# A two-layer encoder trunk on one core: activation tables fetched in place, the squares of x four chunks later, and two more matmul steps for two joins

## The chip, the cores and the metric

The kernel runs on one core of one Trainium2 chip. The metric is the device time of one execution in microseconds; less is better. A profile of one execution is read beside it. The engines are named as in the profile: PE multiplies matrices (PEld loads its weights), DVE works on vectors, ACT evaluates activation functions and copies with a scale, POOL works on vectors too, and SP issues most transfers from the chip's memory.

## The reference

The input is one sequence of 512 tokens with 1024 features. Two layers follow each other, and each adds a mixer and then an MLP to the stream x, both in sandwich form:

```
x = x + RMSNorm_post(mixer(RMSNorm_pre(x)))
x = x + RMSNorm_post(mlp(RMSNorm_pre(x)))        mlp(h) = relu(h @ w1)**2 @ w2, hidden 4096
layer 0 mixer: short gated convolution and latent attention with 8 heads, one input and one output projection
layer 1 mixer: u = h @ w_pw1 + b; u = a * sigmoid(g); depthwise convolution, width 31;
               LayerNorm over channels; silu; @ w_pw2 + b
```

All arithmetic is float32 to the outside.

## The kernel before

The activations lie transposed: eight chunks of 128 features on the partitions, tokens along the row. A weight strip of 128x1024 comes in by SP, is split into a rounded part `whi` (ACT, line 224) and a remainder `wlo` (POOL, line 225), and each product takes three matmuls, high by high, high by low and low by high (lines 247 to 249, `mm`), so that one output tile of 128 features takes 8 chunks x 3 = 24 matmuls. Only two raw strips are held at the start, and eight split strips, so SP issues a strip when POOL has finished an older one, and ACT splits one when PE has finished with the strip eight before it.

**The start.** `split_x(j)` loads chunk j of x, multiplies it by its gain on DVE (line 572), splits the product into h (ACT, line 231) and its remainder (DVE, line 234), and has ACT square x for the norm (`square`, line 359); DVE adds the squares up (line 334). `START` interleaves this with the first weight strips. The matmuls don't wait for the norm: PE sums 512-token products in five PSUM banks (`S` has three, `pj` two), and each result is multiplied by R0, the broadcast reciprocal root, when it leaves its bank (line 604). R0 comes from a sum over partitions on PE (line 369), a Newton iteration on DVE (`rstd`, lines 395 to 425), a broadcast on PE (`spread`, line 434) and a copy by ACT (line 596).

**The later stages.** From the first MLP on, the tokens are worked on in two halves, A and B, that are out of step with each other: while one half passes through a join or a norm, in which PE would wait, the other half's matmul steps are pulled forward. The lists `M2` and `M3` give the order by hand. A step is one output tile (24 matmuls); `('down', 'B', 0, 0, 0, 2)` stands for the steps 0 and 1 of a down projection. `hold` and `pace`, called inside a join or a norm, pull the next step from the list, but only as long as it belongs to the other half:

```
        if not steps or steps[0][0] or steps[0][1][1] in ("F", scope["half"]):
            return False
```

So the join `('join', 'A', 0, 3)` can pull the ten steps that stand behind it, eight of up and two of down of half B, and then meets `('pw1', 'A', ...)`, which is its own half's. Pulled steps don't call for convolution work (`fill` returns at once while pulling); every other step gives credit to the convolution taps that DVE works off between other things, 2.6 us for a first down step.

A **join** (`join`) takes the post norm, adds to x, sums squares, takes `rstd`, broadcasts it by `spread` (PE, line 434) and makes the next input h: product on DVE (line 505), rounded copy on ACT (line 231), remainder on DVE (line 234). The **gated units** `pw1` follow (`glu`): two output tiles each, sigmoid of the second (ACT, line 801), product on DVE into u (line 805), which frees the first one's bank. The **norm** (`layer_norm`) first uses up what is left of the convolutions, then sums, broadcasts the mean (line 434), sums squares (line 369), broadcasts the reciprocal root (line 434), and makes h again: product (DVE, line 860), silu (ACT, line 863), rounded copy (ACT, line 231), remainder (DVE, line 234). `pw2` multiplies that.

ACT holds one table of functions at a time; a function that isn't in it needs an ACT_TABLE_LOAD first, which the compiler puts ahead of it. Copy, square and relu appear behind any of the loads in this kernel. To fetch tables early, `join` and `layer_norm` run sigmoid and silu on a 128x1 tile `warm` (lines 502 and 848), which depends on nothing but a memset at the program's start.

The order of each engine's instructions is set by the framework's scheduler from the dependences and its own estimate of durations; for DVE from `M2` on it is the order in which the code was written.

## Time and profile before

| | |
|---|---|
| median of three runs | 1176.1 us (1175.84 to 1176.19) |
| the profiled execution, its own time | 1176.2 us |
| its span from first to last instruction | 1174.4 us |
| PE busy, of the span | 1135.2 us, 97% |
| ACT, DVE, POOL busy | 667.8, 648.6 and 846.6 us |
| mean granted PE clock | 0.991 |

The profiled execution's time agrees with the median to 0.1 us; 1.8 us of it lie outside the span. The page's first part gives busy times by engine. The view of waits names who waited for whom, with the sum, the number and the longest in microseconds. In a timeline, a row has its start, its duration, engine, line, operation and tiles, and in brackets the idle time of the engine ahead of it and what ended that. The view by stretches gives each engine's busy time in a stretch with the number of instructions, then the granted PE clock, the share of the DMA engines and their GB/s.

### The profile page before, as it was taken

What the parts mean: (1) busy time and instruction counts of PE and PEld (TensorE: products, weight loads), DVE (VectorE), ACT (ScalarE), POOL (GpSimd) and SP (SyncE); (2) the same over time, 40 slices, a digit from 0 to 9 for tenths busy, and PEclk for the clock granted to TensorE, in tenths of its full rate; (3) what the DMA queues carried; (4) which work ended last, traced back from release to release, by engine and by line L of the source; (5) the groups of instructions that cost most, each with busy time, mean ns of one, the idle gap of its engine ahead of it and who ended that gap; (6) DMA issues with size and microseconds to landing.
All of it is one profiled execution on the core that took longest, in us unless ns stands there. A gap on an engine that the chain in (4) does not pass through costs nothing.

```text
span 1174.4 us, 22870 instructions
## 1 busy us (share of the span) xinstructions
PE 1135.2 (97%) x8850; PEld 1096.5 (93%) x8850; DVE 648.6 (55%) x1701; ACT 667.8 (57%) x1220; POOL 846.6 (72%) x409
## 2 busy tenths in 40 slices
PE   6999989999999999999999999999999999999995
PEld 4888879999999999899999999899999999999995
DVE  5652699554522124599965265699975272322123
ACT  7521667556845457545566678546467685545352
POOL 4664553148988888688886878698888877877681
PEclk9999999999999999999999999999999999999998
DMA  6421332037655555455554655455555555653431
GB/s 193 157 89 36 97 108 72 1 105 240 200 180 190 188 173 189 135 201 184 179 195 147 200 178 184 139 200 197 197 177 183 179 172 170 197 180 127 156 130 39
DMA packets 55405, 184.00 MB, mean 157 GB/s; under 512 B 6400, under 2 KB 10880, under 8 KB 55296
## 3 DMA queue, kind: packets, MB, share of 16 engines
q1 hardware_dynamic: 54720, 181.86, 46.8%
q8 instruction: 69, 1.13, 0.4%
q10 hardware_dynamic: 576, 0.68, 0.2%
q14 instruction: 40, 0.33, 0.1%
HBM read 180.42 MB, written 2.10 MB: 155 GB/s over the span
## 4 chain that ended last, share of the span: by engine, by line
PE 86%; ACT 4%; DVE 4%; POOL 2%; DMA 2%; issue 1%; POOLq 0%; ACTq 0%; DVEq 0%
PE S L247 22%; PE S L248 21%; PE S L249 21%; PE pj L247 6%; PE pj L248 6%; PE pj L249 6%; POOL wlo L225 2%; DMA raw<-in_w 1%; ACT whi L224 1%; DVE pr L763 1%; PE mi L369 1%; PE mi L434 1%; PE mi L766 1%; PE o L248 1%; DVE s L757 1%
## 5 line engine op out<-in xcount | busy, mean ns | idle before, releaser
L225 POOL TENSOR_TENSOR wlo<-raw,whi 128x1024 fp32r<-128x1024 f32 (+2 forms) x347 | 803.5, 2330 | 258.2 <-ACT whi L224 249.6
L224 ACT ACTIVATE whi<-raw 128x1024 fp32r<-128x1024 f32 (+2 forms) x347 | 355.9, 1031 | 378.0 <-PE S L248 173.1
L247 PE MATMUL S<-h,whi 128*128 128x256 f32 (+3 forms) x1208 | 347.3, 290 | 5.5 <-ACT h L231 3.7
L248 PE MATMUL S<-h,whi 128*128 128x256 f32 (+3 forms) x1208 | 348.4, 289 | 0.0
L249 PE MATMUL S<-h,wlo 128*128 128x256 f32 (+3 forms) x1208 | 348.3, 289 | 0.0
L247 PEld LDWEIGHTS S<-h,whi 128*128 128x128 f32 x1208 | 227.8, 190 | 10.8 <-ACT h L231 4.3
L247 PE MATMUL S<-hid,whi 128*128 128x256 f32 (+2 forms) x824 | 230.3, 282 | 2.3 <-DVE acc L334 1.8
L249 PEld LDWEIGHTS S<-h,wlo 128*128 128x128 f32 x1208 | 229.1, 190 | 3.5
L248 PEld LDWEIGHTS S<-h,whi 128*128 128x128 f32 x1208 | 228.9, 190 | 3.5 <-issue 0.2
L248 PE MATMUL S<-hid,whi 128*128 128x256 f32 (+2 forms) x824 | 230.9, 281 | 0.0
L249 PE MATMUL S<-hid,wlo 128*128 128x256 f32 (+2 forms) x824 | 230.4, 281 | 0.0
L828 DVE SCALAR_TENSOR_TENSOR pj<-u,taps,pj 128x240 f32<-128x240 f32 (+1 forms) x464 | 190.9, 483 | 1.0
L247 PEld LDWEIGHTS S<-hid,whi 128*128 128x128 f32 x824 | 154.8, 189 | 3.3 <-DVE acc L334 2.2
L249 PEld LDWEIGHTS S<-hid,wlo 128*128 128x128 f32 x824 | 155.6, 189 | 0.0
L248 PEld LDWEIGHTS S<-hid,whi 128*128 128x128 f32 x824 | 155.5, 189 | 0.1
L247 PE MATMUL pj<-h,whi 128*128 128x272 f32 (+3 forms) x344 | 105.8, 308 | 11.9 <-ACT h L231 10.2
L248 PE MATMUL pj<-h,whi 128*128 128x272 f32 (+3 forms) x344 | 105.1, 306 | 0.5 <-DVE h L234 0.5
L249 PE MATMUL pj<-h,wlo 128*128 128x272 f32 (+3 forms) x344 | 104.5, 304 | 0.0
L247 PEld LDWEIGHTS pj<-h,whi 128*128 128x128 f32 x344 | 64.9, 189 | 15.7 <-ACT h L231 11.0
L237 DVE TENSOR_TENSOR hid<-S,hid 128x256 fp32r<-128x256 f32 (+2 forms) x102 | 42.8, 420 | 54.3 <-ACT hid L231 54.0
L248 PEld LDWEIGHTS pj<-h,whi 128*128 128x128 f32 x344 | 65.0, 189 | 4.2 <-DVE h L234 1.8
L249 PEld LDWEIGHTS pj<-h,wlo 128*128 128x128 f32 x344 | 65.0, 189 | 2.6
(250 smaller groups left out, 1661.7 us busy)
## 6 DMA issues: line engine op xcount, KB each, us to landing
raw<-in_w SPq DMA_DIRECT2D x256, 512.0 KB, 3.3
raw<-in_pw SPq DMA_DIRECT2D x48, 512.0 KB, 3.4
raw<-in_win SPq DMA_DIRECT2D x16, 512.0 KB, 3.3
x<-in_xT SPq DMA_DIRECT2D x16, 256.0 KB, 4.6
raw<-in_wout SPq DMA_DIRECT2D x8, 512.0 KB, 3.3
raw<-in_wq SPq DMA_DIRECT2D x8, 192.0 KB, 2.3
out<-x SPq DMA_DIRECT2D x8, 120.0 KB, 3.1
out<-x SPq DMA_DIRECT2D x5, 136.0 KB, 1.7
```

The costliest lines, as they stand in the source:

```text
L224: nc.scalar.activation(h, r, AF.Copy)
L225: nc.gpsimd.tensor_tensor(out=lo[:, c0:c1], in0=r, in1=h.bitcast(F32), op=ALU.subtract)
L237: eng.tensor_tensor(out=lo, in0=src, in1=hi.bitcast(F32), op=ALU.subtract)
L247: nc.tensor.matmul(acc, sh, mh, start=i == 0, stop=False)
L248: nc.tensor.matmul(acc, sh, ml, start=False, stop=False)
L249: nc.tensor.matmul(acc, sl, mh, start=False, stop=i == n - 1)
L369: nc.tensor.matmul(s[:, b : b + 1], q[:, sl.start - self.seg.lo : sl.stop - self.seg.lo], one, start=i == 0, stop=i == len(self.parts) - 1,)
L434: nc.tensor.matmul(o[:, sl], r[:, b : b + 1].to_broadcast([bw, P]), ident[:bw, :bw], start=True, stop=True,)
L757: nc.vector.reduce_max(out=mx, in_=S, axis=AX.X)
L763: eng.tensor_scalar(out=pr_, in0=pr_, scalar1=sm, scalar2=None, op0=ALU.mult)
L766: nc.tensor.transpose(tp[:, kb * P : (kb + 1) * P], pr_[:, kb * P : (kb + 1) * P], ident)
L828: nc.vector.scalar_tensor_tensor(out=dst, in0=src, scalar=wk, in1=acc, op0=ALU.mult, op1=ALU.add)
```

## The change

Three edits go together.

1. The tile `warm` is gone. A fetch of a table writes a new small tile and reads one column of a sum or of the mean that was made just ahead of it, so it can't be placed before that value exists.
2. In the start, chunk j's call squares chunk j-4, and the last four are squared behind all chunks; the sum of squares for R0 is therefore issued later, and the splits of x come first.
3. In `M2`, the first down group of half B stands with four steps ahead of `('pw1', 'A', 0, 8)` and four behind, and the first down group of half A in layer 1 likewise around `('pw1', 'B', 0, 8)`; before it was two and six.

```diff
-... ('down', 'B', 0, 0, 0, 2), ('pw1', 'A', 0, 8), ('down', 'B', 0, 0, 2, 8), ...
-... ('down', 'A', 1, 0, 0, 2), ('pw1', 'B', 0, 8), ('down', 'A', 1, 0, 2, 8), ...
+... ('down', 'B', 0, 0, 0, 4), ('pw1', 'A', 0, 8), ('down', 'B', 0, 0, 4, 8), ...
+... ('down', 'A', 1, 0, 0, 4), ('pw1', 'B', 0, 8), ('down', 'A', 1, 0, 4, 8), ...
+LAG = 4
+    def table():
+        return new(sp, "table", 2, 1)
 # join
         bc = rstds(ssq)
-        nc.scalar.activation(warm[0], warm[0], AF.Sigmoid)
+        nc.scalar.activation(table(), ssq.parts[0][:, :1], AF.Sigmoid)
 # split_x
-        s0.square(xs[j].t)
+        if j >= LAG:
+            s0.square(xs[j - LAG].t)
 # behind the loop over START
     settle()
+    for j in range(NC - LAG, NC):
+        s0.square(xs[j].t)
+        settle()
 # layer_norm
         total = spread(mu, seg)
-        nc.scalar.activation(warm[0], warm[0], AF.Silu)
+        nc.scalar.activation(table(), mu[:, :1], AF.Silu)
 # ahead of run(M2)
-    warm.append(new(sp, "warm", 1, 1))
-    nc.vector.memset(warm[0], 0.0)
```

Lines up to 445 are one higher in the changed kernel, those of `join` and `split_x` five, those of the start behind it and of `layer_norm` nine.

On ACT at the program's start, before (its first four rows stand there twice, one set behind the other) and after; `ycat` is the square of the first chunk, `mi` and `o` are scaled chunks, `x3` the second chunk of x:

```order
L502 ACT_TABLE_LOAD
L502 ACTIVATE warm596_2837<-warm596_2837 128x1
L848 ACT_TABLE_LOAD
L848 ACTIVATE warm596_2837<-warm596_2837 128x1
L359 ACTIVATE ycat27_107<-x2_79 128x512
L224 ACTIVATE whi29_110<-raw28_109 128x128
L231 ACTIVATE h10_87<-mi26_104 128x512
```

```order
L567 ACT_TABLE_LOAD
L567 ACTIVATE s11_75<-s11_75 128x1
L360 ACTIVATE ycat37_151<-x2_79 128x512
L225 ACTIVATE whi28_108<-raw27_107 128x128
L232 ACTIVATE h10_87<-mi26_104 128x512
L225 ACTIVATE whi28_108<-raw27_107 128x896
L225 ACTIVATE whi32_122<-raw31_121 128x256 x2
L232 ACTIVATE h12_89<-o30_117 128x512
```

In the kernel before, all four fetches stood at the program's start, ahead of the first square; they are gone from there, and the other squares come behind the splits of the first five chunks.

On ACT in the join of half A behind the first MLP, where `m` is half B's down sum taken out of its bank `S`, and `h` the first chunk of the joined half, before and after:

```order
L231 ACTIVATE hid1003_5258<-S1057_5589 128x256
L224 ACTIVATE whi1091_5815<-raw21090_5814 128x1024
L533 ACTIVATE m487_2157<-S1066_5643 128x256
L224 ACTIVATE whi1094_5821<-raw1093_5820 128x1024
L533 ACTIVATE m488_2158<-S1075_5694 128x256
L231 ACTIVATE h503_2181<-o1068_5673 128x256
```

```order
L232 ACTIVATE hid1002_5256<-S1056_5587 128x256
L507 ACT_TABLE_LOAD
L507 ACTIVATE table1067_5670<-acc11021_5359 128x1
L225 ACTIVATE whi1089_5801<-raw21088_5800 128x1024
L538 ACTIVATE m487_2157<-S1065_5641 128x256
L225 ACTIVATE whi1092_5807<-raw1091_5806 128x1024
L538 ACTIVATE m488_2158<-S1075_5693 128x256
L225 ACTIVATE whi1099_5878<-raw1098_5877 128x1024
L538 ACTIVATE m489_2159<-S1082_5737 128x256
L232 ACTIVATE h503_2181<-o1068_5672 128x256
```

The fetch of the sigmoid's table now stands in the join, and a third down step with its strip comes ahead of h. On PE that step's 24 matmuls stand directly ahead of the broadcast; the fourth step stands behind the units' first matmuls. In the join of half B (the one ahead of its gated units) both steps stand around the broadcast: 33 of their matmuls ahead of it, 15 behind.

On PE in the norm of half A, at the broadcast of the reciprocal root (`mi<-kst,s`), before and after; `hid` are steps of half B, `h` the norm's own output:

```order
L249 MATMUL S1369_7808<-hid1287_7280,wlo1342_7632 128x256
L434 MATMUL mi1357_7749<-kst_70,s21351_7703 128x128 x2
L247 MATMUL S1376_7855<-hid1273_7266,whi1346_7668 128x256
L248 MATMUL S1376_7855<-hid1274_7267,whi1346_7668 128x256
L249 MATMUL S1376_7855<-hid1273_7266,wlo1347_7669 128x256
```

```order
L250 MATMUL S1382_7904<-hid1287_7266,wlo1355_7728 128x256
L435 MATMUL mi1370_7845<-kst_70,s21364_7799 128x128 x2
L248 MATMUL S1390_7958<-h503_2181,whi1359_7764 128x240
L248 MATMUL S1395_7992<-h503_2181,whi1367_7814 128x240
L249 MATMUL S1390_7958<-h504_2182,whi1359_7764 128x240
```

Before, two steps of half B (48 matmuls) stood between the broadcast and the first matmul on h, and a third behind that one's first 13; now the first matmul on h follows the broadcast at once, and four tiles of `pw2` take turns chunk by chunk. In the norm of half B one step stands between (three before). At the start, the broadcast of R0 stood 49 matmuls of 512 columns ahead of the first use of the sixth strip; now it stands directly ahead of it, behind all 120 matmuls of the first five.

## The prediction

> **What bounds the kernel now.** I read the page first, then the view of waits for PE, then PE's timeline around each wait, and last the view by stretches, for the clock.

> ```profile
> span 1174.4 us, 22870 instructions
> PE 1135.2 (97%) x8850; PEld 1096.5 (93%) x8850; DVE 648.6 (55%) x1701; ACT 667.8 (57%) x1220; POOL 846.6 (72%) x409
> PE pj L247 <- ACT h L231: 10.2, 2, 9.5
> ```

> PE is the bound. The change removes no matmul, so it can act only on what PE loses: waits, of which the largest is 9.5 us at the start (the third row: sum, number, longest), and time at a reduced clock. The columns of the next view are the stretch, the sum, busy time and number for PE, PEld, DVE, ACT and POOL, then the granted clock, the DMA share and GB/s.

> ```profile
> 477.37:480.78 3.41, 1.65 (x11) 1.42 (x12) 2.44 (x9) 2.65 (x7) 3.04 (x2) 1.00 0.00 0
> 480.78:484.20 3.42, 3.42 (x19) 3.42 (x18) 3.24 (x10) 1.69 (x5) 1.65 (x1) 0.50 0.67 206
> 484.20:487.61 3.41, 3.41 (x31) 3.41 (x31) 1.18 (x4) 0.52 (x2) 0.00 (x0) 1.00 0.28 106
> 634.38:637.79 3.41, 1.97 (x18) 1.78 (x16) 1.37 (x5) 3.38 (x8) 3.19 (x2) 1.00 0.29 113
> 637.79:641.20 3.41, 3.08 (x23) 2.89 (x24) 2.14 (x7) 1.66 (x5) 1.52 (x1) 1.00 0.70 231
> 736.78:740.20 3.42, 1.57 (x12) 1.22 (x11) 2.25 (x12) 2.74 (x5) 2.09 (x1) 1.00 0.30 119
> 740.20:743.61 3.41, 3.19 (x15) 3.19 (x16) 3.23 (x9) 1.68 (x5) 2.60 (x2) 0.50 0.48 154
> ```

> A clock change lands on a grid of 3.41 us. Where PE was busy 1.65 or 1.57 us of a stretch, the next one runs at 0.50; after 1.97 us it stays at 1.00. A full stretch holds 31 matmuls, so one takes 0.11 us. The two halved stretches lose 31 - 19 = 12 matmuls, 1.3 us, and 31 - 16 = 15, 1.65 less the 0.2 us of wait in it, about 1.45. Both lie right behind the two joins that the change touches.

> **The start.** Rows of the timeline, and the transfer of x (KB, then median us to landing):

> ```profile
> 2.25 1.28 ACT L502 ACT_TABLE_LOAD   x1
> 3.93 0.75 DVE L572 TENSOR_SCALAR mi<-x,vec 128x512 f32<-128x512 f32 x1 [3.04 <-DMA x<-in_xT]
> 8.20 0.61 ACT L359 ACTIVATE ycat<-x 128x512 f32<-128x512 f32 x1
> 8.91 0.57 ACT L231 ACTIVATE h<-mi 128x512 fp32r<-128x512 f32 x1
> 9.54 0.79 PE L247 MATMUL pj<-h,whi 128*128 128x512 f32 x1 [9.54 <-ACT h L231]
> 13.25 0.40 PE L249 MATMUL pj<-h,wlo 128*128 128x512 f32 x1
> 20.11 1.72 PE L369 MATMUL mi<-kst,ycat 128*128 128x1 f32 x14
> 35.11 0.58 ACT L596 ACTIVATE R<-mi 128x512 f32<-128x512 f32 x1
> 35.72 0.69 DVE L604 TENSOR_TENSOR ycat<-pj,R 128x512 f32<-128x512 f32 x1 [7.00 <-ACT R L596]
> 45.14 0.48 PE L247 MATMUL pj<-h,whi 128*128 128x512 f32 x1
> 18.40:45.10 26.70, 26.58 (x130) 21.94 (x130) 17.36 (x34) 14.79 (x21) 19.02 (x8) 1.00 0.41 135
> x<-in_xT SPq DMA_DIRECT2D x16, 256.0 KB, 4.6
> ```

> Four pairs of a table load and a tiny activation hold ACT from 2.25 to 8.20. Chunk 0 of x is there by 3.9 (the DVE row), so without them the square of chunk 0, a small split and h can follow: the first matmul moves from 9.54 to about 4.7 + 0.6 = 5.3.

> PE can't keep those 4.2 us, because x comes no earlier: a transfer lands 4.6 us after its issue, SP issues as before, and the later chunks wait for theirs. By my count from their landings some 14 matmuls are done at 13.2, against 7 before the row at 13.25. In full flow a 512-column matmul takes 0.23 us (the stretch 18.40 to 45.10: 26.58 us less some 3.5 for 26 short ones, over 104), so seven more are worth 1.6 us. Between 13.25 and the sixth strip's first matmul at 45.14 PE has 31.9 us, of which 113 matmuls take 26.1 and the short ones (the 1.72 row and two broadcasts and sums of about 0.8) 3.2; the other 2.6 us are waits for h and whi before about 18.4, which should mostly go, since ACT squares five chunks later and the splits come first.

> Against that stands R0. Its broadcast now comes behind all 120 matmuls, when all five banks are full, so PE waits for ACT's copy and DVE's first product: 0.58 + 0.69 and some 0.15 of handing over, 1.45 us. Before, 49 matmuls (11 us) covered it. That gives -1.6 - 2.6 + 1.45 = -2.75. I take **-2.5**, a little less because the copy stands behind the split of a late strip. The ends: -0.6 if only the wait for R0 is new and half of the early waits stay, -4.25 if R0 costs nothing. The sine's own table load of 1.28 us, which silu's load used to spare, falls into a stretch where PE has no wait, and the cover is the 26.58 us of PE work out of 26.70; bare it would be 1.28.

> **The joins and the units behind them.**

> ```profile
> 478.13 0.71 PE L434 MATMUL mi<-kst,s 128*128 128x128 f32 x4 [0.91 <-DVE s L420]
> 479.84 0.62 PE L247 MATMUL S<-h,whi 128*128 128x256 f32 x3 [1.00 <-ACT h L231]
> 490.55 1.06 ACT L224 ACTIVATE whi<-raw 128x1024 fp32r<-128x1024 f32 x1 [0.94 <-PE pj L248]
> 491.63 1.28 ACT L801 ACT_TABLE_LOAD   x1
> 492.92 0.47 ACT L801 ACTIVATE y<-pj,vec 128x256 f32<-128x256 f32 x1
> 493.43 0.48 DVE L805 SCALAR_TENSOR_TENSOR u<-S,vec,y 128x256 f32<-128x256 f32 x1 [7.92 <-ACT y L801]
> 493.97 0.39 PE L247 MATMUL S<-h,whi 128*128 128x256 f32 x1 [0.92 <-DVE u L805]
> 738.74 0.68 PE L434 MATMUL mi<-kst,s 128*128 128x128 f32 x4 [1.07 <-DVE s L420]
> 740.42 0.79 PE L247 MATMUL S<-h,whi 128*128 128x256 f32 x2 [1.00 <-ACT h L231]
> 753.84 0.38 PE L247 MATMUL S<-h,whi 128*128 128x256 f32 x1 [0.40 <-ACT y L801]
> ```

> Each join has a wait for the Newton root ahead of the broadcast and one for h behind it. Behind half A's sum 24 more matmuls (2.6 us) now stand ahead of the broadcast: the 0.91 goes. The wait for h gets another strip split (1.06) ahead of it on ACT, but DVE's chain is the longer part; I put it at 1.15, +0.15. With about 2.3 us busy in the stretch the clock should stay up: -1.3. Join A: **-2.1**; ends -0.8 (clock halves anyway) and -3.2 (both waits go).

> In half B's join 33 matmuls (3.6 us) stand ahead of the broadcast and 15 (1.65 us) behind it, so both waits go, 1.07 + 1.00, and the halved stretch, 1.45: **-3.5**; ends -1.1 and -3.6.

> Each moved step takes its strip along: SP's transfer, ACT's split and POOL's remainder stand earlier than those of half B's or A's unit strips behind them, in the same order as the steps. POOL needs 846.6/409 = 2.1 us for one instruction, less than a step's 24 x 0.11 = 2.65 on PE, which is the cover; so I cost the strips at nothing. Without the cover a strip would come late by about one split, 1.06 in each join, which the ends hold.

> What is late next is the gated units: their first product now has fewer matmuls beside it. The chain from the last matmul of the gate is split 1.06, sigmoid 0.47, product 0.48, with gaps some 2.4 us; beside it stand 10 matmuls (1.1 us), before 21 in half A and 29 in half B. In half A the load of 1.28 goes from this chain, into the join, and so the wait stays about 1.0 where it was 0.92: **0**, ends -0.9 and +0.4. In half B the wait grows from 0.40 to about 1.1: **+0.7**, ends -0.4 and +1.0.

> [...]

> **The norms.**

> ```profile
> 629.96 1.28 ACT L863 ACT_TABLE_LOAD   x1
> 631.26 0.56 ACT L863 ACTIVATE pj<-m,vec 128x240 f32<-128x240 f32 x1
> 632.23 0.35 ACT L231 ACTIVATE h<-pj 128x240 fp32r<-128x240 f32 x1
> 638.05 0.38 PE L247 MATMUL S<-h,whi 128*128 128x240 f32 x1 [1.70 <-ACT h L231]
> 640.33 0.37 ACT L231 ACTIVATE h<-mi 128x240 fp32r<-128x240 f32 x1
> 892.70 0.58 ACT L863 ACTIVATE pj<-m,vec 128x272 f32<-128x272 f32 x1
> 900.55 0.38 PE L247 MATMUL pj<-h,whi 128*128 128x240 f32 x1 [1.46 <-DVE h L234]
> 903.01 0.40 ACT L231 ACTIVATE h<-o 128x272 fp32r<-128x272 f32 x1
> ```

> Two steps fewer behind the units give 2 x 2.6 us less credit to the convolutions, so more of them is done inside the norm, under pulled steps. In norm A these run out at the last broadcast; nothing stands between it and h. The load of 1.28 goes there as well. What is left is DVE's product (about 0.4), silu to h 632.23 - 631.26 = 0.97, h 0.35 and a bit of a strip's split: about 2.0 us where 1.70 was, **+0.3**. Ends +1.2 (the whole split of 1.06 ahead) and -1.7. In norm B one step covers the first chunks, and I put the waits at 1.9 instead of 1.46, **+0.4**; ends +1.5 and -1.4.

> Sum: -2.5 - 2.1 - 3.5 + 0 + 0.7 + 0.3 + 0.4 = -6.7. The profiled execution took 1176.2 us, its span and 1.8 around it, 0.1 above the median of 1176.1: 1169.5 by its own time, and against the median **1169.4**.

> **The rivals.**

> *Clock again.* A 2.0 us wait in norm A that lies wholly in one stretch leaves 1.4 us busy, under the 1.57 that halved. Whether it does hangs on where the grid falls, about evenly. It costs another 1.4: 1170.8.

> [...]

> *The start gives nothing.* Transfers of x and strips set the pace to 18 us and R0 takes the rest: 1169.4 + 2.5 = 1171.9. For it speaks that DVE already waits for x at 3.93; against it the 2.6 us of waits behind 13.25, when x has landed. [...]

> *R0 is hidden.* If another bank is free, the start keeps 4.25: 1167.6.

> *Slower: the norms run at the pace of their chunks.* From the first silu to the last h 9.4 us pass in half A (631.26 to 640.70) and 10.7 in half B (892.70 to 903.41). If PE could use each chunk for one tile only, 24 x 0.11 = 2.65 us, it would idle 6.8 and 8.1, against 1.7 and 1.46 now: 1169.4 - 0.7 + 11.7 = 1180.4. It decides when the norms together lose more than 9 us beyond the forecast's. Against it: four tiles take turns on each chunk, 96 x 0.11 = 10.6 us of work for 9.4 us of chunks.

> **How the numbers follow.** Chances: forecast 0.40, clock again 0.20, halved stretches stay 0.08, start gives nothing 0.10, start and clock 0.06, no change 0.05, R0 hidden 0.06, slower 0.05. About 0.2%, 2.35 us, is what a measurement here tells from no change, so faster means under 1173.75. No change and slower lie outside, start and clock (1173.3) by half: faster 0.40 + 0.20 + 0.08 + 0.10 + 0.06 + 0.03 = 0.87, same 0.03 + 0.05, slower 0.05. The range 1166.0 to 1173.8 goes from R0 hidden, with the join ends, to start and clock; it leaves out some 0.15.

> **What the changed profile would show.** PE's first matmul near 5.3; a new wait of about 1.5 for the R0 product near 42; no wait ahead of the two broadcasts that waited 0.91 and 1.07, and 1.00 as the clock behind them; a wait near 1 at both first units; about 2 in norm A. Six loads on ACT in front of sigmoid, silu, sine and exp outside the start, none of them with PE waiting. The prediction is wrong if the first matmul stays behind 8 us, if clock 0.50 stands in a stretch with more than 2 us of work before it, or if a norm's waits sum to over 4 us.

## The result, and the profile after

The changed kernel takes 1168.4 us (median of four runs, 1166.52 to 1169.85) against 1175.97 (1174.64 to 1176.19): a ratio of 0.9937, 95% interval 0.992 to 0.9954, 7.6 us less. The forecast was 1169.4. In the set with the experiments it was run again: 1167.65 against 1174.61, 0.9942 (0.993 to 0.9954). One execution of the kernel without fetches (below), at 6373 us, is left out of its figures.

The page of the profiled execution, and its view of waits:

```profile
span 1164.6 us, 22863 instructions
PE 1132.3 (97%) x8850; PEld 1093.1 (94%) x8850; DVE 645.7 (55%) x1696; ACT 663.8 (57%) x1221; POOL 846.2 (73%) x409
PE pj L248 <- ACT h L232: 5.5, 1, 5.5
PE S L248 <- ACT h L232: 3.4, 3, 1.8
```

The rows of the timeline that answer to those of before, in the order of time: the first matmul, R0's copy and product and the wait for them, then the waits at join A, first unit A, norm A, first unit B and norm B:

```profile
5.47 0.80 PE L248 MATMUL pj<-h,whi 128*128 128x512 f32 x1 [5.47 <-ACT h L232]
41.64 0.69 DVE L613 TENSOR_TENSOR ycat<-pj,R 128x512 f32<-128x512 f32 x1 [5.53 <-ACT R L605]
42.39 0.50 PE L248 MATMUL pj<-h,whi 128*128 128x512 f32 x1 [1.41 <-DVE ycat L613]
477.73 0.62 PE L248 MATMUL S<-h,whi 128*128 128x256 f32 x3 [1.18 <-ACT h L232]
493.06 0.38 PE L248 MATMUL S<-h,whi 128*128 128x256 f32 x1 [0.79 <-DVE u L814]
632.86 0.49 PE L248 MATMUL S<-h,whi 128*128 128x240 f32 x2 [1.85 <-ACT h L232]
749.11 0.39 PE L248 MATMUL S<-h,whi 128*128 128x256 f32 x1 [0.78 <-DVE u L814]
897.72 0.52 PE L248 MATMUL S<-h,whi 128*128 128x272 f32 x2 [0.34 <-ACT h L232]
```

There is no row of a wait ahead of a broadcast in either join any more, and none for h in join B. The clock, in the stretch with join A's wait and the one behind it, and at norm A:

```profile
475.44:478.85 3.41, 2.23 (x18) 2.00 (x17) 2.02 (x6) 2.16 (x5) 3.41 (x3) 1.00 0.44 149
478.85:482.26 3.41, 3.41 (x31) 3.41 (x30) 3.10 (x10) 1.64 (x5) 2.07 (x1) 1.00 0.56 175
629.03:632.44 3.41, 1.99 (x18) 1.79 (x16) 1.42 (x5) 1.90 (x3) 3.00 (x2) 1.00 0.52 167
632.44:635.85 3.41, 2.99 (x24) 2.84 (x25) 2.93 (x9) 2.59 (x8) 1.60 (x1) 1.00 0.64 204
```

In this pair of executions PE's n-th matmul starts earlier than before by

| n | 500 | 1000 | 3100 | 4300 | 5300 | 6000 | 7200 | 8800 |
|---|---|---|---|---|---|---|---|---|
| us | 1.85 | 2.85 | 3.97 | 6.70 | 6.70 | 10.13 | 10.15 | 9.74 |

The first column is the start. Between the third and the fourth lie join and first units of half A, between the fourth and the fifth its norm; the next two hold the same of half B. Two gains were in no term of the forecast: 1.0 us in the attention between 500 and 1000, where the execution of before had a stretch at half clock (from 156.52, behind one in which PE was busy 1.51 us) and this one has none, and 1.1 us between 1000 and 3100, where PE waits for next to nothing. And the two norms gain nothing, though the row of norm B's wait is 1.1 us shorter than before.

### The profile page after: what moved, and what is told of

It reads as the page before. It is cut to its first block, busy times and chain, and to the rows that moved or that the text cites. A ratio compares the mean times of both kernels' runs of the same rounds, so it can differ in the third digit from the quotient of the medians.

```text
span 1164.6 us, 22863 instructions
## 1 busy us (share of the span) xinstructions
PE 1132.3 (97%) x8850; PEld 1093.1 (94%) x8850; DVE 645.7 (55%) x1696; ACT 663.8 (57%) x1221; POOL 846.2 (73%) x409
## 4 chain that ended last, share of the span: by engine, by line
PE 92%; DVE 3%; ACT 3%; DMA 1%; issue 1%; POOL 0%; SPq 0%; POOLq 0%; ACTq 0%
PE S L248 23%; PE S L249 23%; PE S L250 22%; PE pj L248 7%; PE pj L249 7%; PE pj L250 7%; DVE pr L772 1%; PE mi L370 1%; PE mi L435 1%; ACT whi L225 1%; PE mi L775 1%; DVE s L766 1%; PE o L249 1%; PE o L250 0%; DVE pt L238 0%
## 5 line engine op out<-in xcount | busy, mean ns | idle before, releaser
L248 PE MATMUL S<-h,whi 128*128 128x256 f32 (+3 forms) x1216 | 346.8, 289 | 6.2 <-ACT h L232 3.4
L249 PE MATMUL S<-h,whi 128*128 128x256 f32 (+3 forms) x1216 | 349.8, 289 | 0.1
L248 PEld LDWEIGHTS S<-h,whi 128*128 128x128 f32 x1216 | 227.5, 189 | 12.2 <-ACT h L232 4.2
L249 PEld LDWEIGHTS S<-h,whi 128*128 128x128 f32 x1216 | 229.4, 189 | 4.3 <-DVE h L235 0.5
L248 PE MATMUL S<-hid,whi 128*128 128x256 f32 (+2 forms) x824 | 230.3, 282 | 2.0 <-DVE acc L335 1.8
L249 PE MATMUL S<-hid,whi 128*128 128x256 f32 (+2 forms) x824 | 230.7, 281 | 0.0
L248 PEld LDWEIGHTS S<-hid,whi 128*128 128x128 f32 x824 | 154.5, 189 | 2.8 <-DVE acc L335 2.2
L249 PEld LDWEIGHTS S<-hid,whi 128*128 128x128 f32 x824 | 155.4, 189 | 0.2 <-DVE hid L238 0.2
L248 PE MATMUL pj<-h,whi 128*128 128x272 f32 (+3 forms) x336 | 103.6, 308 | 6.9 <-ACT h L232 5.5
L249 PE MATMUL pj<-h,whi 128*128 128x272 f32 (+3 forms) x336 | 103.1, 307 | 0.0
L248 PEld LDWEIGHTS pj<-h,whi 128*128 128x128 f32 x336 | 63.7, 190 | 10.1 <-ACT h L232 5.8
L540 DVE TENSOR_TENSOR m<-S,m 128x256 f32<-128x256 f32 (+2 forms) x74 | 30.6, 416 | 65.3 <-PE S L250 65.3
L249 PEld LDWEIGHTS pj<-h,whi 128*128 128x128 f32 x336 | 63.6, 189 | 3.4 <-DVE h L235 0.9
## 6 DMA issues: line engine op xcount, KB each, us to landing
x<-in_xT SPq DMA_DIRECT2D x16, 256.0 KB, 4.2
```

What stands on the lines that cost most here:

```text
L248: nc.tensor.matmul(acc, sh, mh, start=i == 0, stop=False)
L249: nc.tensor.matmul(acc, sh, ml, start=False, stop=False)
L540: nc.vector.tensor_tensor(out=m[seg.sl], in0=acc, in1=m[seg.sl], op=ALU.add)
```

## Experiments

Theory A is the forecast's: each edit acts by the waits of PE that it removes or makes, and a load of 1.28 us counts where it lies in a chain without cover. The rivals stand with each run. Changes in us are the ratio times 1174.5.

### Each edit alone

**Only the fetches in place.**

```diff
-LAG = 4
+LAG = 0
-... ('down', 'B', 0, 0, 0, 4), ('pw1', 'A', 0, 8), ('down', 'B', 0, 0, 4, 8) ...
-... ('down', 'A', 1, 0, 0, 4), ('pw1', 'B', 0, 8), ('down', 'A', 1, 0, 4, 8) ...
+... ('down', 'B', 0, 0, 0, 2), ('pw1', 'A', 0, 8), ('down', 'B', 0, 0, 2, 8) ...
+... ('down', 'A', 1, 0, 0, 2), ('pw1', 'B', 0, 8), ('down', 'A', 1, 0, 2, 8) ...
```

The diff is against the changed kernel.

> Only the first edit: the fetches read a value made in the join or the norm; squares and steps as before. Theory A (every edit acts by the waits it removes, and a fetch in place takes its load of 1.28 us out of the chains of the gated units and of the norms too): PE's first matmul at 5.5 us; R0's broadcast keeps its 49 matmuls of cover, so no wait of 1.4; the waits of 0.92 and 0.40 at the first units go; the norms' 1.70 and 1.46 shrink by up to 1.3 each; both halved stretches behind the joins stay, since the waits 0.91 + 1.00 and 1.07 + 1.00 stay. In sum -4 to -6 us against before. Theory B (the fetches cost something at the start only): -1.5 to -2.5 us, with the waits at units and norms unchanged.

Measured: 0.9954 (0.9941 to 0.9968), -5.4 us. Its timeline at the joins and norms:

```profile
475.15 0.71 PE L435 MATMUL mi<-kst,s 128*128 128x128 f32 x4 [0.90 <-DVE s L421]
476.86 0.62 PE L248 MATMUL S<-h,whi 128*128 128x256 f32 x3 [1.00 <-ACT h L232]
631.75 0.38 PE L248 MATMUL S<-h,whi 128*128 128x240 f32 x1 [1.42 <-ACT h L232]
733.98 0.68 PE L435 MATMUL mi<-kst,s 128*128 128x128 f32 x4 [1.07 <-DVE s L421]
893.35 0.38 PE L248 MATMUL pj<-h,whi 128*128 128x240 f32 x1 [0.93 <-DVE h L235]
```

The joins' waits are as before; both unit waits (0.92 and 0.40) are gone, and the norms' have shrunk from 1.70 to 1.42 and from 1.46 to 0.93. PE's 500th matmul is 2.06 us earlier, all of the start. Theory A holds, with two reservations. The norms gave 0.8 us and not up to 2.6. And 1.1 of the 5.4 us are not theory A's: they lie between matmul 1000 and 3100, where PE has no wait (below, the unused tile). In this execution neither stretch behind the joins ran at half clock, though their waits stayed.

**Only the later squares** (fetches as before, two steps).

Against the kernel before:

```diff
+LAG = 4
...
-        s0.square(xs[j].t)
+        if j >= LAG:
+            s0.square(xs[j - LAG].t)
...
+    for j in range(NC - LAG, NC):
+        s0.square(xs[j].t)
+        settle()
```

> Only the second edit: squares four chunks later; the fetches stay in a block at the start, steps as before. Theory A: the block of fetches still holds ACT until 8.2, so the first matmul stays near 9.5; the splits of x come first and save up to 2 us of early waits, and the wait for R0 (1.4) appears: -0.7 to +1.0 us in sum. Theory B (the order of squares against splits is what gains at the start): -2 us, with the fetches harmless.

Measured: 1.0001 (0.9991 to 1.001): nothing, as by theory A. The first matmul stands at 9.54 as before, the early waits are gone, and one row is new:

```profile
43.78 0.53 PE L248 MATMUL pj<-h,whi 128*128 128x512 f32 x1 [1.41 <-DVE ycat L613]
```

**Only the steps** (fetches and squares as before).

Against the kernel before:

```diff
-... ('down', 'B', 0, 0, 0, 2), ('pw1', 'A', 0, 8), ('down', 'B', 0, 0, 2, 8) ...
-... ('down', 'A', 1, 0, 0, 2), ('pw1', 'B', 0, 8), ('down', 'A', 1, 0, 2, 8) ...
+... ('down', 'B', 0, 0, 0, 4), ('pw1', 'A', 0, 8), ('down', 'B', 0, 0, 4, 8) ...
+... ('down', 'A', 1, 0, 0, 4), ('pw1', 'B', 0, 8), ('down', 'A', 1, 0, 4, 8) ...
```

> Only the third edit: four steps ahead of the units in place of two; fetches and squares as before. Theory A: the joins' waits (0.91, 1.07, 1.00) and both halved stretches go, -5.6, but the units' load of 1.28 now lies in a chain with 10 matmuls beside it, not 21 and 29: wait at half A's first unit 2.2 in place of 0.92, at half B's 2.4 to 2.6 in place of 0.40, and 3 us in place of 1.70 at norm A: +1.3, +2.1, +1.5, perhaps with a halved stretch of 1.4 behind one of them: -2 to +1 us in sum. Theory B (the steps are worth their 5 us by themselves): -4.5 to -6 us.

Measured: 1.0045 (1.0032 to 1.0057), 5.3 us slower, outside both theories. The first unit of half A, norm A, the first unit of half B:

```profile
495.09 1.28 ACT L801 ACT_TABLE_LOAD   x1
497.43 0.38 PE L247 MATMUL S<-h,whi 128*128 128x256 f32 x1 [2.21 <-DVE u L805]
640.47 0.49 PE L247 MATMUL S<-h,whi 128*128 128x240 f32 x2 [3.27 <-ACT h L231]
757.30 1.28 ACT L801 ACT_TABLE_LOAD   x1
759.63 0.39 PE L247 MATMUL S<-h,whi 128*128 128x256 f32 x1 [2.21 <-DVE u L805]
```

and the stretches with these three waits, each with the next:

```profile
494.36:497.77 3.41, 1.20 (x11) 0.99 (x10) 0.79 (x2) 3.38 (x5) 3.41 (x2) 1.00 0.64 177
497.77:501.18 3.41, 3.41 (x19) 3.41 (x18) 3.16 (x8) 1.34 (x3) 3.41 (x3) 0.50 0.74 270
637.72:641.13 3.41, 0.66 (x4) 0.52 (x5) 1.23 (x4) 3.38 (x8) 2.34 (x1) 1.00 0.48 154
641.13:644.54 3.41, 3.41 (x18) 3.41 (x18) 2.58 (x9) 2.59 (x8) 0.00 (x0) 0.50 0.47 159
757.19:760.60 3.41, 1.21 (x11) 1.00 (x10) 1.43 (x3) 3.38 (x5) 3.41 (x2) 1.00 0.24 72
760.60:764.01 3.41, 3.41 (x19) 3.41 (x18) 3.20 (x8) 0.72 (x2) 3.41 (x3) 0.50 0.66 240
```

The waits came out as worked out (2.2, 3, 2.4), but the sum did not: behind all three (PE busy 1.20, 0.66 and 1.21 us of the stretch) the clock stood at 0.50 for a stretch, where theory A had put one such stretch as a perhaps. Norm B, which the working left out, takes PE 142.3 us from the start of its matmul 6000 to that of its matmul 7200, and 140.8 before. And the joins' two halved stretches, which theory A took as gained, are in part chance, as the runs below show. So the same edit that costs 5.3 us alone gains about 1.9 on top of the fetches in place (0.9954 with the fetches, 0.9938 with both, below; the ratios' intervals overlap, the executions, 1168.3 to 1170.1 us and 1166.6 to 1167.9, don't). The load of 1.28 us makes the difference twice, as itself and by the clock: with it in the chain the waits are 2.21, 3.27 and 2.21 and half clock follows each, without it 0.79, 1.85 and 0.78 in the changed kernel's first profile, and none follows.

### Pairs, and the changed kernel without one edit

**Fetches and squares, two steps.** The last diff backwards, on the changed kernel.

> First and second edit together, steps as before. Theory A: as with the fetches alone, but the early waits between 13 and 18 us go and the wait of 1.4 for R0 comes: within 1 us of the run with the fetches alone. Theory B (the two edits need each other at the start, the squares being what gains once ACT is free): 1.5 to 2.5 us better than the fetches alone.

Measured: 0.9964 (0.995 to 0.9977), -4.2 us against -5.4 for the fetches alone, a difference that the two intervals leave open. Theory A; the squares don't gain once ACT is free.

**Fetches and steps, squares at once.**

```diff
-LAG = 4
+LAG = 0
```

> The changed kernel without its second edit (each chunk squared at once, as before). Theory A (the later squares gain the early waits and pay them back as the wait of 1.41 for R0): PE's first matmul still at 5.5; one early wait of about 1.6 and one of 0.4 in place of 0.7 and 1.41; within 0.5 us of the changed kernel in the same set of runs. Theory B (the later squares carry part of the gain): 1.5 us or more slower than the changed kernel.

Measured: 0.9938 (0.9926 to 0.995), 1167.35 us against 1167.65 for the changed kernel. Its two early waits are the expected ones, and R0 has its cover back:

```profile
9.23 0.80 PE L248 MATMUL S<-h,whi 128*128 128x512 f32 x1 [1.63 <-ACT whi L225]
15.40 0.51 PE L248 MATMUL pj<-h,whi 128*128 128x512 f32 x1 [0.47 <-ACT h L232]
```

1.63 + 0.47 here (and a third of 0.21), 0.71 + 1.41 in the changed kernel's first profile: the second edit moves the wait. In the changed kernel's second profile the two are 1.35 and 1.73, and its 500th matmul starts 0.6 us later than in the first.

**The changed kernel again**, beside these.

> The changed kernel itself, in the same set of runs: 0.993 to 0.995 of before. By theory A a stretch at half clock behind norm A appears in some executions and not in others (its wait of 1.85 us may fall into one stretch of 3.41 or into two), so single executions differ by about 1.4 us or twice that.

Measured: 0.9942 (0.993 to 0.9954). Its profile has no stretch at half clock behind norm A, as the first one had none. But it has one in the attention, behind waits of the same length as in the first profile, which has none there. The two stretches of this execution, then those of the first:

```profile
152.36:155.77 3.41, 1.43 (x8) 1.02 (x9) 3.41 (x8) 0.95 (x2) 3.25 (x3) 1.00 0.45 154
155.77:159.19 3.42, 3.42 (x17) 3.32 (x17) 3.35 (x6) 1.67 (x5) 1.12 (x1) 0.50 0.37 98
151.16:154.57 3.41, 1.60 (x11) 1.08 (x9) 3.41 (x6) 1.55 (x2) 3.25 (x4) 1.00 0.48 154
154.57:157.99 3.42, 3.14 (x22) 2.63 (x21) 3.38 (x7) 2.25 (x5) 1.98 (x1) 1.00 0.13 24
```

So one program halves its clock at a place in one execution and not in the next, as theory A has it, here at another place than norm A.

### The start with cover for R0, and three steps

**Squares one chunk behind.**

```diff
-LAG = 4
+LAG = 1
```

> The changed kernel with the squares one chunk behind in place of four. R0's broadcast then stands 14 matmuls of 512 columns (3.2 us) ahead of the sixth strip, and the splits of the first two chunks still come ahead of the next square. Theory A (R0's 1.41 us is a matter of cover): no wait for R0, early waits of about 0.7 to 1.0: 0.7 to 1.4 us faster than the changed kernel. Theory B (the wait only moves, because the chain behind R0 is late with fewer matmuls done): no difference, within 0.3.

Measured: 0.9932 (0.9918 to 0.9947), 1166.98 us. The sixth strip's first matmul:

```profile
40.73 0.50 PE L248 MATMUL pj<-h,whi 128*128 128x512 f32 x1 [0.56 <-DVE ycat L613]
```

It starts at 40.73, in the changed kernel at 42.39, and PE's 500th matmul stays 1.63 us ahead. In the whole the difference is 0.7 us and not told apart from nothing. The profiled execution lost 1.65 us again in norm A: the same wait of 1.85 us stands there in both kernels; here it lies in one stretch of the grid, and in the second execution of the changed kernel it is spread over two:

```profile
629.55:632.96 3.41, 1.56 (x11) 1.34 (x11) 2.52 (x8) 3.38 (x9) 2.69 (x2) 1.00 0.51 154
632.96:636.38 3.42, 3.42 (x18) 3.42 (x17) 2.59 (x8) 2.63 (x8) 0.00 (x0) 0.50 0.48 158
```

```profile
630.22:633.64 3.42, 2.70 (x24) 2.51 (x22) 1.72 (x8) 1.68 (x3) 2.45 (x2) 1.00 0.43 153
633.64:637.05 3.41, 2.29 (x18) 2.14 (x18) 2.58 (x9) 2.89 (x8) 2.30 (x1) 1.00 0.55 169
```

(first the kernel with one chunk, then the changed kernel.) Half of theory A stands, then: with more cover R0's wait shrinks to 0.56, and in the two further kernels with one chunk, below, to 0.30 and to nothing.

**The same with three steps ahead of half A's units.**

```diff
-... ('down', 'B', 0, 0, 0, 4), ('pw1', 'A', 0, 8), ('down', 'B', 0, 0, 4, 8) ...
+... ('down', 'B', 0, 0, 0, 3), ('pw1', 'A', 0, 8), ('down', 'B', 0, 0, 3, 8) ...
```

> As the run before, and three steps (in place of four) ahead of half A's units; half B keeps four. In half A one step still stands between the sum and the broadcast, so the wait of 0.91 stays away; beside the first unit's product stand 15 matmuls in place of 10. Theory A (the first unit's wait is its chain of 2.1 us less its cover): wait at half A's first unit 0.79 - 5 x 0.117 = 0.2; 0.5 to 0.8 us faster than the run before. Theory B (the fourth step pays for itself elsewhere, in the norm's cover): no faster, norm A's wait 0.4 or more longer.

Measured: 0.9942 (0.9929 to 0.9955), 1166.87 us, no faster. The wait at the first unit is 0.63, not 0.2: 15 matmuls of cover were not 5 x 0.117 better than 10. Its row no longer names DVE's product but ACT's sigmoid, and on ACT two strip splits (2.01 us) stand ahead of that. Norm A's wait fell to 0.95, against theory B, and norm B's, which had been 0.34, came back as four waits of 0.49, 0.76, 0.96 and 0.32, two of them for DVE's sums of half A's steps. From the start of matmul 6000 to that of 7200, around norm B, PE takes 143.2 us, against 140.8 with four steps. Neither theory foresaw that one step of half A moves half B's norm.

**One chunk behind, and more credit for the first down steps.**

```diff
-FILL = {'up': 2.3, 'down': 2.3, 'first': 2.6, ...
+FILL = {'up': 2.3, 'down': 2.3, 'first': 4.2, ...
```

> As the run with the squares one chunk behind, and each first down step gives 4.2 us of credit to the convolutions in place of 2.6, which gives back what the two lost steps gave. The order then has 48 matmuls of half B between norm A's last broadcast and the first matmul on h, and 24 in norm B, as before the change. Theory A (the norm's wait follows the pace of its chunks, not this cover): waits as with the fetches alone, 1.4 in norm A and 0.9 in norm B, in sum within 0.4 us of the 1.85 + 0.34 without the credit; no more than 0.5 us faster than with the squares one chunk behind alone. Theory B (what the steps cost is the norms' cover): both norm waits under 0.5, 1.5 us or more faster.

Measured: 1.0043 (1.0026 to 1.006), 5 us slower, as neither theory had it. The norms' waits are theory A's, 1.42 and 0.93. But PE now waits 4.1 and 6.2 us, each time three up steps behind the four first down steps that give the credit, and runs at half clock for two stretches behind each:

```profile
544.50:547.91 3.41, 0.36 (x4) 0.15 (x2) 3.38 (x10) 2.29 (x5) 2.98 (x2) 0.99 0.65 225
547.91:551.33 3.42, 2.35 (x11) 2.35 (x12) 3.42 (x10) 0.00 (x0) 0.40 (x1) 0.50 0.56 178
551.33:554.74 3.41, 3.41 (x18) 3.41 (x18) 3.41 (x10) 0.40 (x1) 0.00 (x0) 0.51 0.00 0
```

DVE (third busy time) is full in all three. From 526.7 to 548.5 it does almost only convolution work, in its written order, ahead of the product (line 238) that lets PE go on at 548.98. A step takes PE 24 x 0.117 = 2.8 us; 4.2 us of taps don't fit beside it.

### The fetch itself, and the 1.1 us without a wait

**No fetch at all**, neither at the start nor in place; against the kernel with the fetches alone:

```diff
-        nc.scalar.activation(table(), ssq.parts[0][:, :1], AF.Sigmoid)
...
-        nc.scalar.activation(table(), mu[:, :1], AF.Silu)
```

> The kernel before without any fetch: neither at the start nor in the joins and norms; squares and steps as before. Theory A (a fetch in place gains twice, by the free start and by taking the load out of the chains): the start's 2.1 us stay gained, but the load of 1.28 stands again in the chain of the first units (waits 0.92 and 0.40) and of the norms (1.70 and 1.46): 1 to 3 us faster than before, 2 to 3.5 slower than the fetches in place. Theory B (all of it is the free start): as fast as with the fetches in place, -5.

Measured: 0.9967 (0.9954 to 0.9979), -3.9 us, 1.5 us less of a gain than in place, though the two intervals overlap. Theory A has the waits right, but both its sizes are missed: 3.9 is more than its 1 to 3, and 1.5 less than its 2 to 3.5. The load is back in the unit's chain:

```profile
484.85 1.07 ACT L225 ACTIVATE whi<-raw 128x1024 fp32r<-128x1024 f32 x1 [0.94 <-PE pj L249]
485.93 1.28 ACT L809 ACT_TABLE_LOAD   x1
488.27 0.38 PE L248 MATMUL S<-h,whi 128*128 128x256 f32 x1 [0.92 <-DVE u L813]
```

The waits of 0.92, 0.40, 1.65 and 1.47 add up to 2.1 us more than those with fetches in place. By the profiles, then, the first edit's 5.4 us are three parts: 2.1 that the block at the start is gone, 2.1 that the fetches stand where they help, and 1.1 of the stretch without a wait, which comes next. The kernel without any fetch has 0.7 of these 1.1, which is a part of why it gains more than theory A gave it.

**The kernel before with one more unused 128x1 tile.**

```diff
     nc.vector.memset(warm[0], 0.0)
+    pad = new(sp, "pad", 1, 1)
+    nc.vector.memset(pad, 0.0)
```

> The kernel before with one more unused 128x1 tile beside the fetches' own. It asks for the 1.1 us that the profiles with the fetches in place gain between matmul 1000 and 3140 (252.3 us in place of 253.4, without a wait in it). Theory A (later tiles lie at other addresses, and matmuls that read them run about 1 ns shorter): 252.3 here as well. Theory B (it has to do with the fetches or with the tables): 253.4. For the time as a whole, within 1.5 us of before.

Measured: 1172.4 us, one run, 2.4 us below the median of before in its set and within that kernel's spread. The stretch from PE's matmul 1000 to 3140 in the kernel before, the changed one and this one:

```profile
213.60:467.05 253.45, 253.42 (x2141) 253.18 (x2141) 97.29 (x285) 147.47 (x288) 188.80 (x96) 1.00 0.51 168
```

```profile
210.76:463.07 252.31, 252.28 (x2141) 252.04 (x2141) 97.28 (x285) 147.21 (x288) 188.85 (x96) 1.00 0.51 168
```

```profile
213.63:465.96 252.33, 252.30 (x2141) 252.06 (x2141) 97.28 (x285) 147.34 (x288) 188.89 (x96) 1.00 0.51 168
```

2141 matmuls without a wait take 253.4, 252.3 and 252.3 us. The squares alone and the steps alone, which keep `warm` as the only such tile, take 253.4; all kernels with the new tile, which has two buffers, or with the unused one beside `warm`, 252.3; with no such tile at all it is 252.75. So none, one and two small buffers give 252.75, 253.4 and 252.3 us: theory B is out, since the fetches of this kernel stand at the start as before, and more tiles are not simply better. That they act by the addresses of later tiles, theory A, fits, and was not shown by itself.

## Why the prediction was right, point by point

The time lay within 1.0 us of the forecast, and start, joins and units went as it said: the waits named went, and the new ones came where they were put. The norms did so only in part, one gain was in no term, and a part of the sum was the chance of an execution's clock. Taken singly, the terms were less good than the sum, whose nearness is in part luck.

- **Start, -2.5: measured -1.85.** First matmul 5.47 (forecast 5.3), 14 matmuls by 13.2 as counted, and the wait for R0 1.41 (1.45). What failed is "the other 2.6 us are waits, which should mostly go": about 1.7 of it went (1.6 + 1.7 - 1.4 = 1.85 or so), and the rows of before mark only 0.46 + 0.70 + 0.22 = 1.4 us of it as PE's waits. The sixth strip itself starts 2.75 us earlier, but eight short matmuls that stood ahead of it now come later, 0.9 us. In this execution the matmuls of 512 columns followed each other every 0.43 us until 14.6 us and every 0.23 from there, in that of before every 0.23 from 13.2 on. The later changes of the clock lie whole stretches of 3.41 us behind that: 13.16 + 42 x 3.413 = 156.52, where the attention's halved stretch of before begins. In the second profile of the changed kernel it rose at 12.4, 41 of these stretches ahead of the row at 152.36. The forecast gave the start to two edits; the runs give it to the first alone, and nothing to the second.
- **Join A, -2.1.** The waits are -0.91 and 1.00 to 1.18, as forecast (1.15). The 1.3 for the halved stretch is no fixed term. With the waits of 0.91 and 1.00 unchanged, the clock halved behind them in the kernel before and with the squares alone, and did not with the fetches alone, with fetches and squares, without fetches, or with the unused tile. Its size was about right: from matmul 3100 to 4300 PE takes 147.6 us before and 146.2 in the kernel with the unused tile, which has the same waits there and no halved stretch.
- **Join B, -3.5.** Both waits went, as forecast; the halved stretch is by chance here too, and cost 1.3 (from matmul 5300 to 6000 85.9 us before, 84.5 with the unused tile).
- **Units, 0 and +0.7.** 0.79 and 0.78, forecast 1.0 and 1.1: -0.13 and +0.38. The cover step was right, the chain a little shorter.
- **Norms, +0.3 and +0.4.** Norm A's wait is 1.85, forecast 2.0; from matmul 4300 to 5300 PE takes 118.7 us before and after, so even the +0.3 isn't seen. Norm B's row fell from 1.46 to 0.34, where 1.9 was forecast, but that is no gain of 1.1: from matmul 6000 to 7200, around this norm, PE takes 140.8 us before and after, since nine of the matmuls on h between 894.0 and 898.5 us follow the one ahead 0.1 to 0.3 us later than the usual 0.125, most without a row of their own. With the fetches alone, where the row is 0.93, it is 140.4. So the steps do cost 0.4 here, as forecast. What failed is the step that left out that the load of 1.28 also leaves this norm's chain, a gain of 0.4.
- **Not in the sum:** 1.1 us by the small tile, and 1.0 by the halved stretch in the attention.

The kernel with the unused tile also tells the joins' waits from their clock: its 146.2 and 84.5 us for join and units of half A and half B stand against 144.8 and 82.4 in the changed kernel, 1.4 and 2.1 us by waits, of which the rows mark 0.7 and 1.7 (the forecast's terms without the clock, units included, were 0.8 and 1.35). Start, tile and these make 1.85 + 1.1 + 1.4 + 2.1 = 6.5 us. The other 3.2 of this pair of executions are the three stretches at half clock in the execution of before, 1.0 in the attention and 1.3 in each join, with none in that of after ahead of the end, less 0.4 lost again behind matmul 7200, which no run explains. It follows that the base was mis-sized as well. The three times of before in the forecast, 1175.8 to 1176.2, lay at the high end: in the later sets the executions of before with a mean clock of 0.991 took 1175.3 to 1176.5 us, those of 0.994 1172.5 to 1173.7, and those of 0.996 1171.5 to 1171.6. A median of 1174.5 would have been the better base, and the clock's part of the gain smaller than 2.75. So the forecast's sum held too much for the clock and nothing for the tile, and the two errors helped each other out.

Of the rivals, *clock again* is real and a matter of each execution: norm A's stretch halved in two of the four profiles that have its wait of 1.85 us (squares at once; one chunk behind), and in neither of the changed kernel. *The halved stretches stay* did not come: both join stretches keep the full clock in both profiles of the changed kernel. *R0 is hidden* needs another number of chunks: with one, 0.56, 0.30 and 0 us are left in three kernels. *The norms run at the pace of their chunks* did not come. *The start gives nothing* fell with the fetches alone.

A single wait was enough for half clock: 2.21 us ahead of the first unit of either half in the steps-only kernel. By PE's busy time in a stretch at full clock, away from the program's two ends, the stretches read here sort like this. With 0.36 us (more credit), 0.66, 1.20 and 1.21 us (the steps alone), 1.43 (the changed kernel again), 1.50 (the squares alone), 1.51 and 1.57 (before) and 1.56 (one chunk behind) the next stretch ran at half clock. With 1.60 (the changed kernel) it did not, with 1.65 (before) and 1.93 (the fetches alone, and the fetches and squares) it did. With 1.97 (before), 1.99 and 2.23 (the changed kernel) and 2.29 (the same again) it did not. Why 1.60 kept the clock and 1.93 did not was not shown.

## What to carry to other kernels

Price an edit together with the others: moving work out of a chain's cover is a gain only when the chain is short, and here the same two steps cost 5.3 us with a table load in the chain and gained about 2 without it. Check a shorter wait by the time from one matmul to a later one: norm B's row lost 1.1 us, and PE's time there did not change. An activation that fetches a table belongs behind a value that exists only where the fetch is wanted; left without a dependence it was issued at the program's start, where four of them held everything behind them (PE's first matmul at 9.54 us, and at 5.47 with the fetches in place). When a wait is moved, look for the work that now has to cover the next one, and count a wait as itself and, where it leaves PE busy 1.57 us or less of a stretch of 3.41, another 1.0 to 1.6 us, as in the profiles here; with 1.60 to 1.93 it was so in some of them.
